# A third staging tile for the spilled pieces of u and of the gates, and accumulating transfers cut at 4 KB instead of 8 KB

## The chip, the cores and the metric

The kernel runs on 1 core of one Trainium2 chip. The metric is the time of one execution in device microseconds (us). Engines are named as the profile names them: PE multiplies, PEld is its weight load, DVE, ACT and POOL compute, and SP only queues transfers. ACT and POOL queue transfers too; such rows read ACTq and POOLq, or DMA_DIRECT2D on POOL. All transfers share 16 DMA engines.

## The reference

One decoder block on 1024 tokens of width 1024, with 16 meta tokens put ahead. All in float32:

```python
h = rmsnorm(concat([meta, x]), norm_g)
u_pool, z_pool, q, k, v, z_attn, f_logit, g_pool, g_attn = split(h @ w_in)
y_pool = causal_multiscale_pool(u_pool, pool_w, pool_scale) * silu(z_pool)
log_f = log_sigmoid(f_logit + b_forget)
y_attn = forgetting_attention(q, k, v, log_f) * silu(z_attn)   # 8 heads of 64, causal
merged = sigmoid(g_pool) * (y_pool @ w_up_pool) + sigmoid(g_attn) * (y_attn @ w_up_attn)
out = rmsnorm(x + merged @ w_out, final_norm_g)
```

## The kernel before, in words

Every product is made of three products of rounded parts (high with high, high with low, low with high), so PE has three matmuls for each. PE's order is written out by hand; the order on the other engines comes from a scheduler.

From about 60 to 430 us the kernel runs 16 attention units (4 head pairs, 2 heads, 2 halves of 512 queries). A unit's scores go through `qk`, then `maxes` takes the maximum over the keys (line 726): DVE transposes the running maxima into the tile `mt` (line 729), reduces it, and a few small copies and one more transposition spread the result; then `soft` exponentiates block by block and `av` multiplies with V. `finish` (line 778) copies the unit's sum into the tile `t`, and SP stores its two halves in DRAM (`sp_y`, line 788). For the last head pair one half is stored.

Between these matmuls PE works off "fill": projections of the input, 24 matmuls to a piece, in chunks of 128 output columns. The projections of q, k and v stay on the chip. Those of u (`f_u`, 4 chunks of 3 pieces) and of 12 gate chunks (`f_raw`, 2 pieces each) are spilled: ACT copies the piece from PSUM into a staging tile `st` of the pool `stg`, which has two, and SP stores it (`sp_u`, `sp_gp`, `sp_ga`). A piece can go into a staging tile only when the store of the piece before last has landed. Fill pieces alternate between two PSUM banks, so a bank must be emptied before the piece after next begins.

Meanwhile sums of blocks of the input and of the weights are made in DRAM by transfers alone. ACT queues copies from DRAM to DRAM (`move`, line 605, rows with `td` and `gs`), one or two of them between the exponentials of a unit; POOL queues transfers that add one DRAM block to another (`add` and `add_y`, lines 614 and 641), 17 transfers of 0.5 to 1.5 MB each, 18.35 MB in all.

Each transfer that SP or ACT queues has one of eight completion semaphores (DMAHW0 to DMAHW7 in the program's rows), dealt out in turn; the queueing engine first waits until the transfer that had this one before, eight transfers back, has landed.

From about 430 us on PE multiplies without a break (products of sums of blocks, then the up and output projections). At that point `F.drain()` has run the last fill pieces, the attention pools are closed, and new tiles (`bp`) take their place.

Of the kernel before, what the change touches and what calls it, by code (L numbers as in the profile page):

```python
# [8 lines left out]
F32 = mybir.dt.float32  # L9
F32R = mybir.dt.float32r  # L10
AF = mybir.ActivationFunctionType
ALU = mybir.AluOpType
# [10 lines left out]
KB = 128  # L23
# [30 lines left out]
def tile_hybrid_block(ctx, tc, x, meta, norm_g, w_in, b_forget, pool_w, pool_scale,  # L54
                      w_up_pool, w_up_attn, w_out, final_g, out):
    nc = tc.nc
# [19 lines left out]
    stg = ctx.enter_context(tc.tile_pool(name="stg", bufs=2))  # L76
# [3 lines left out]
    ap_ = A.enter_context(tc.tile_pool(name="ap", bufs=1))  # L80
# [36 lines left out]
    def behind(ins, prev):  # L117
        tc.add_manual_dep(ins.ins, prev.ins.name,
                          mybir.DependencyInfo(mybir.DependencyClass.Sync, mybir.DependencyReason.DATA),
                          reason="wait")  # L120
# [41 lines left out]
    def w_chunk(col, **kw):  # L162
        return split_w([w_in2[:, :, col:col + 128]], **kw)
# [20 lines left out]
    def g_proj(w, t0, t1):  # L184
        wh, wl = w
        ps = fill_bank()[:, :t1 - t0]
        yield from g_mm3(ps, [(wh[:, k, :], wl[:, k, :], hh[k][:, t0:t1], hl[k][:, t0:t1]) for k in range(KO)])
        return ps
# [69 lines left out]
    def keys_of(t0, t1):  # L258
        r = [(0, min(t1, SEQ) - t0, t0 + NM)]
        if t1 > SEQ:  # L260
            r.append((SEQ - t0, t1 - t0, 0))
        return [(slice(a, b), slice(d, d + b - a)) for a, b, d in r]
# [72 lines left out]
            if c0:  # L335
                yield from v_blocks(p, *{384: (1, 2), 768: (3, 4, 5)}[c0])

    spill, stores, evacs = {}, [], []

    def f_raw(key, col):  # L340
        w = w_chunk(col)
        dt = dr.tile([128, SEQ], F32, name=f"sp_{key[0]}{key[1]}")
        spill[key] = dt
        for c0, c1 in HALVES:
            ps = yield from g_proj(w, c0, c1)
            st = stg.tile([128, 512], F32, name="st")
            evacs.append(nc.scalar.activation(st, ps, AF.Copy))
            stores.append(nc.sync.dma_start(dt[:, c0:c1], st))

    def f_u(g):  # L350
        w = w_chunk(COL_U + g * 128)
        dt = dr.tile([128, L], F32, name=f"sp_u{g}")
        spill["u", g] = dt
        for c0, c1 in PIECES:
            ps = yield from g_proj(w, c0, c1)
            st = stg.tile([128, 512], F32, name="st")[:, :c1 - c0]
            nc.scalar.activation(st, ps, AF.Copy)
            for c, d in keys_of(c0, c1):
                last = nc.sync.dma_start(dt[:, d], st[:, c])
            stores.append(last)  # L360

    class Fill:
# [3 lines left out]
        def add(self, name, g, gate=0, apart=False):  # L366
            self.must.append((name, g, gate, apart))
# [245 lines left out]

    def add(dst, src):
        d, r = [t.rearrange("r c -> (r c)").rearrange("(p m) -> p m", m=2048) for t in (dst, src)]
        behind(nc.gpsimd.dma_start(d, r, accum_op=ALU.add, max_dma_last_dim=8192), trs[-1])

    trs = []

# [20 lines left out]

    def add_y(p):
        d, r = [spill[n, p].rearrange("(p k) c -> p (k c)", k=2) for n in ("y", "y2")]
        behind(nc.gpsimd.dma_start(d, r, accum_op=ALU.add, max_dma_last_dim=8192), trs[-1])

    SUMS = {
        0: [(put_h, "11")],
        1: [(add, HS["11"], HS["l11"]), (n21, 0), (put, TD[1], WB["11"]), (put, TD[5], WB["12"])],
        2: [(add, TD[1], TD[5]), (n21, 1), (put_h, "22")],
        3: [(add, HS["22"], HS["l22"]), (n21, 2), (put, TD[3], WB["22"])],
        4: [(add, TD[3], TD[5]), (n21, 3), (put_g, GS[1], GB["11"])],  # L650
        5: [(add, HS["X"], HS["11"]), (n12, 0), (put_g, GS[5], GB["12"])],
# [23 lines left out]
    class Unit:  # L675
# [49 lines left out]

        def maxes(self, extra=0.0, hook=None):
            F.pull(LM1 + extra)
            mt = ap_.tile([KB, 512], F32, name="mt")
            tr = nc.vector.transpose(mt, self.m)
            if hook is not None:  # L730
                hook(tr)
            r, r2 = self.m[:, :16], self.m[:, 16:32]
            x, y, mx = [sm.tile([128, 16], F32, name=n) for n in ("mx", "my", "mz")]
            nc.vector.tensor_reduce(r, mt.rearrange("p (j b) -> p j b", b=32), axis=AX.X, op=ALU.max)
            for a, b in ((0, 64), (64, 0)):
                nc.scalar.activation(x[a:a + 64], r[b:b + 64], AF.Copy)
            nc.vector.tensor_tensor(r2, r, x, op=ALU.max)
            for a, b in ((0, 32), (32, 0), (64, 96), (96, 64)):
                nc.scalar.activation(y[a:a + 32], r2[b:b + 32], AF.Copy)
            nc.vector.tensor_tensor(mx, r2, y, op=ALU.max)  # L740
            self.pm = psT.tile([128, 512], F32, name="pt")
            nc.vector.transpose(self.pm, mx[:, :, None].to_broadcast([128, 16, 32]))
            F.pull(LM2)
# [62 lines left out]
    for g in (3, 2, 1, 0):  # L806
        F.add_free(f_u(g))
    for key in raws:
        F.add_free(f_raw(key, cols[key[0]] + 128 * key[1]))
# [10 lines left out]
    def sums_at(i, tr):  # L820
        trs.append(tr)
        sums_of(i)
        if i % 4 == 1 and i > 1:
            add_y(i // 4 - 1)
# [664 lines left out]
```

## Time and profile before

| what | value |
|---|---|
| time, median of 3 runs | 721.52 us (720.6 to 723.17) |
| the profiled execution's own time | 722.44 us |
| its span in the trace | 720.4 us |
| PE busy | 707.4 us, 98% of the span |
| DVE, ACT, POOL busy | 512.0, 425.9 and 353.9 us |

The span is the time between the first and the last instruction on the chip; 2.0 us of the execution's time lie outside it. A busy time is a sum over an engine's instructions. Where PE is busy nearly all the time, only its gaps, and what sets their ends, can be saved or added to.

### The profile page before, as it was taken

The page shows a single profiled execution, that of the slowest core. Times are in us where ns is not written, and L with a number is a line of the kernel's source. Part 1 is how long each engine was busy: PE and PEld are TensorE (multiplying, and loading weights), DVE is VectorE, ACT ScalarE, POOL GpSimd, SP SyncE. Part 2 cuts the span into 40 slices and gives each one's busy share as a digit, 9 for nine tenths or more (in the row PEclk, how much of TensorE's full clock was granted, in tenths as well). Part 3 has the DMA queues.
Part 4 walks back from the last instruction along what each step waited for, and adds up shares of the span by engine and source line. Part 5 has one row for each costly group of instructions (what it writes and reads, how often), then busy time and mean ns, then how long its engine had stood idle before and what let it go on. Part 6 is the DMA issues. An engine that isn't in the chain of part 4 may idle for free.

```text
span 720.4 us, 10921 instructions
## 1 busy us (share of the span) xinstructions
PE 707.4 (98%) x3613; PEld 610.7 (85%) x3613; DVE 512.0 (71%) x909; ACT 425.9 (59%) x936; POOL 353.9 (49%) x481
## 2 busy tenths in 40 slices
PE   8999999799999999999999999999999999999996
PEld 6997999798889988898888888888888888888885
DVE  5743488477688767787587866899847545888775
ACT  7753577567787867777587614455646332535445
POOL 5412336477377675747388643458951010007152
PEclk9999999999999999999999999999999999999999
DMA  9211225986968889497858768799518366861006
GB/s 308 65 30 30 60 62 199 271 244 193 260 177 230 239 229 281 118 261 214 224 154 206 223 202 318 239 304 308 129 35 273 113 224 233 272 224 60 0 1 233
DMA packets 97482, 134.09 MB, mean 186 GB/s; under 512 B 11809, under 2 KB 63009, under 8 KB 95154
## 3 DMA queue, kind: packets, MB, share of 16 engines
q1 hardware_dynamic: 83296, 94.07, 40.8%
q0 software_dynamic: 2512, 18.35, 13.3%
q10 hardware_dynamic: 11618, 20.98, 8.2%
q8 instruction: 28, 0.46, 0.2%
q14 instruction: 28, 0.23, 0.1%
HBM read 103.29 MB, written 62.59 MB: 230 GB/s over the span
## 4 chain that ended last, share of the span: by engine, by line
PE 94%; ACT 2%; DMA 2%; DVE 1%; issue 1%; POOL 0%; POOLq 0%; ACTq 0%
PE pj L170 55%; PE pj L1049 12%; PE pj L1369 8%; PE po L775 5%; PE pt L1049 4%; PE pt L1369 2%; PE ps L711 2%; DMA sp_u<-st 2%; PE ps L710 2%; PE pj L521 1%; PE pt L232 1%; PE pj L711 1%; PE pj L710 1%; ACT qa L268 1%; PE pn L232 0%
## 5 line engine op out<-in xcount | busy, mean ns | idle before, releaser
L170 PE MATMUL pj<-hh,whi 128*128 128x512 f32 (+3 forms) x576 | 128.3, 350 | 0.0
L170 PE MATMUL pj<-hh,wlo 128*128 128x512 f32 (+3 forms) x576 | 127.1, 346 | 0.0
L170 PE MATMUL pj<-hl,whi 128*128 128x512 f32 (+3 forms) x576 | 126.8, 345 | 0.0
L170 PEld LDWEIGHTS pj<-hh,whi 128*128 128x128 f32 x576 | 98.4, 190 | 10.2 <-ACT hh L234 0.4
L158 POOL TENSOR_TENSOR wlo<-raw,whi 128x256 fp32r<-128x256 f32 x100 | 73.5, 774 | 65.1 <-PE pj L170 24.5
L170 PEld LDWEIGHTS pj<-hh,wlo 128*128 128x128 f32 x576 | 96.8, 188 | 10.0
L765 POOL TENSOR_TENSOR acc<-acc,S 128x256 f32<-128x256 f32 (+2 forms) x128 | 90.3, 723 | 30.5 <-ACT S L752 20.8
L170 PEld LDWEIGHTS pj<-hl,whi 128*128 128x128 f32 x576 | 96.6, 189 | 9.8
L757 DVE TENSOR_TENSOR pl<-S,ph 128x512 fp32r<-128x512 f32 (+4 forms) x112 | 80.5, 736 | 19.4 <-ACT ph L756 18.9
L1011 POOL TENSOR_TENSOR gw<-graw,gw 128x256 fp32r<-128x256 f32 x52 | 53.6, 1056 | 44.2 <-ACT gw L1004 41.8
L1049 PE MATMUL pj<-gh,gw 128*128 128x512 f32 x276 | 64.3, 389 | 0.0
L724 DVE TENSOR_TENSOR pt<-pt,S 128x400 f32<-128x400 f32 (+2 forms) x96 | 46.4, 483 | 22.1 <-ACT S L715 19.6
L1049 PEld LDWEIGHTS pj<-gh,gw 128*128 128x128 f32 x276 | 51.8, 188 | 10.9
L752 ACT ACTIVATE S<-S 128x512 f32<-128x512 f32 (+4 forms) x112 | 50.6, 479 | 8.6 <-DVE S L751 8.4
L756 ACT ACTIVATE ph<-S 128x512 fp32r<-128x512 f32 (+4 forms) x112 | 52.4, 482 | 2.3 <-PE po L775 1.4
L751 DVE TENSOR_TENSOR S<-S,pt 128x512 f32<-128x512 f32 (+4 forms) x112 | 49.7, 498 | 0.6
L1262 DVE TENSOR_TENSOR rl<-pj,rl 128x512 f32<-128x512 f32 x32 | 22.0, 689 | 28.7 <-PE pj L170 28.1
L1004 ACT ACTIVATE gw<-graw 128x512 fp32r<-128x512 f32 x38 | 23.5, 626 | 27.9 <-DMA graw<-gs 12.0
L715 ACT ACTIVATE S<-ps,negc 128x16 f32<-128x16 f32 (+4 forms) x65 | 33.0, 513 | 10.9 <-PE ps L711 10.3
L765 POOL TENSOR_TENSOR acc<-S 128x256 f32<-128x256 f32 (+1 forms) x32 | 28.6, 926 | 21.1 <-ACT S L752 17.5
L136 POOL TENSOR_TENSOR X<-G 128x256 f32<-128x256 f32 x8 | 5.8, 740 | 63.9 <-DVE G L1264 63.9
L775 PE MATMUL po<-ph,V 128*128 128x512 f32 (+4 forms) x112 | 36.6, 327 | 0.3 <-ACT ph L756 0.2
(250 smaller groups left out, 1434.2 us busy)
## 6 DMA issues: line engine op xcount, KB each, us to landing
raw<-in_w_in_dram SPq DMA_DIRECT2D x27, 512.0 KB, 5.9
gs<-in_w_in_dram ACTq DMA_DIRECT2D x15, 512.0 KB, 7.6
gs<-gs POOLq DMA_DIRECT2D x4, 1536.0 KB, 12.7
graw<-gs SPq DMA_DIRECT2D x12, 512.0 KB, 6.1
td<-in_w_out_dram ACTq DMA_DIRECT2D x10, 512.0 KB, 11.4
graw<-in_w_in_dram SPq DMA_DIRECT2D x9, 512.0 KB, 6.9
xt<-in_x_dram SPq DMA_DIRECT2D x8, 512.0 KB, 6.3
accd<-acc SPq DMA_DIRECT2D x16, 256.0 KB, 4.2
```

The source lines that it names most:

```text
L158: ins = nc.gpsimd.tensor_tensor(lo[:, k:k + 2], raw[:, k:k + 2], r32(hi[:, k:k + 2]), op=ALU.subtract)
L170: nc.tensor.matmul(ps, a, b, start=(i == 0), stop=(i == len(seq) - 1))
L724: nc.vector.tensor_tensor(m[:kb, c0:], m[:kb, c0:], s[:kb, c0:], op=ALU.max)
L751: nc.vector.tensor_tensor(s[:kb, c0:], s[:kb, c0:], self.pm[:kb, c0:], op=ALU.subtract)
L752: exps.append(nc.scalar.activation(s[:kb, c0:], s[:kb, c0:], AF.Exp))
L756: nc.scalar.activation(ph[:kb, c0:], s[:kb, c0:], AF.Copy)
L757: dves.append(nc.vector.tensor_tensor(pl[:kb, c0:], s[:kb, c0:], r32(ph[:kb, c0:]), op=ALU.subtract))
L765: accs.append(nc.gpsimd.tensor_tensor(acc[:kb, c:c1], (S0 if b == 1 else acc)[:kb, c:c1], s[:kb, c:c1], op=ALU.add))
L775: nc.tensor.matmul(self.po[:, c0:], v, self.P[b][i][:kb, c0:], start=(b == 0 and i == 0), stop=(b == self.nb - 1 and i == 1))
L1011: nc.gpsimd.tensor_tensor(op[:, 1, k:k + 2], raw[:, k:k + 2], r32(op[:, 0, k:k + 2]), op=ALU.subtract)
L1049: nc.tensor.matmul(ps, stat(n, i, p, k), op_h[n][q][k // 2][:, k % 2], start=fresh and m == 0, stop=m == 11, skip_group_check=True)
L1369: nc.tensor.matmul(ps, pick(A_, k, p)[:, i * 128:(i + 1) * 128], pick(B_, k, q)[:, c0:c1], start=start and n == 0, stop=n == 11, skip_grou ...
```

## The change

The pieces of u and of the gates go through three staging tiles in turn instead of two. The third is a tile of the attention pool `ap`, and its 2 KB per partition come from `mt`, which now shares the buffer of `t` (tag "t"). The transfers that add are cut into pieces of at most 4096 bytes instead of 8192.

```diff
-    spill, stores, evacs = {}, [], []
+    spill, stores, evacs, staged = {}, [], [], [0]
+
+    def stage_in():
+        staged[0] += 1
+        if staged[0] % 3:
+            return stg.tile([128, 512], F32, name="st")
+        return ap_.tile([128, 512], F32, name="st", bufs=1)
...
-            st = stg.tile([128, 512], F32, name="st")
+            st = stage_in()
...
-            st = stg.tile([128, 512], F32, name="st")[:, :c1 - c0]
+            st = stage_in()[:, :c1 - c0]
...
-        behind(nc.gpsimd.dma_start(d, r, accum_op=ALU.add, max_dma_last_dim=8192), trs[-1])
+        behind(nc.gpsimd.dma_start(d, r, accum_op=ALU.add, max_dma_last_dim=4096), trs[-1])
...
-        behind(nc.gpsimd.dma_start(d, r, accum_op=ALU.add, max_dma_last_dim=8192), trs[-1])
+        behind(nc.gpsimd.dma_start(d, r, accum_op=ALU.add, max_dma_last_dim=4096), trs[-1])
...
-            mt = ap_.tile([KB, 512], F32, name="mt")
+            mt = ap_.tile([KB, 512], F32, name="mt", tag="t")
```

Line numbers after the change are 6 higher from `f_raw` on. The order of the instructions on PE, ACT and DVE stays as it was; on POOL only the shape of the adding transfers differs, and on SP one pair of stores moves at the end of the fill. What the instructions wait for does change.

The first place is ACT in the second attention unit, where the last two pieces of the u chunk 1 (`st_1646`, `st_1700`) are staged while the copies `td1` and `td5` are queued. SP's store of `st_1646` stands there in the program like this, before and after, with semaphore 4:

```order
L609 DMA hsX_802<-neg_1671 128x512 [waits DMAHW2_49,Activation_49,Pool_49]
L609 DMA hsA_799<-neg_1671 128x512 [waits DMAHW3_49]
L359 DMA sp_u1_1505<-st_1646 128x384 [waits DMAHW4_49,Activation_49]
L788 DMA sp_y0_773<-t_1728 64x512 [waits DMAHW5_49,Activation_49]
L788 DMA sp_y20_774<-t_1728 64x512 [waits DMAHW6_49]
```

ACT before:

```order
L612 DMA td1_781<-in_w_out_dram 256x512 [waits DMAHW7_49]
L756 ACTIVATE ph_1785<-S_1446 128x400 [waits Activation_49]
L357 ACTIVATE st_1700<-pj_1649 128x272 [waits PE_49]
L752 ACTIVATE S_1550<-S_1550 128x272 [waits DVE_49]
L612 DMA td1_781<-in_w_out_dram 256x512 [waits DMAHW1_49]
L756 ACTIVATE ph_1810<-S_1550 128x272 [waits Activation_49]
L752 ACTIVATE S_1550<-S_1550 128x144 [waits DVE_49]
L612 DMA td5_785<-in_w_out_dram 256x512 [waits DMAHW4_49]
L715 ACTIVATE S_1733<-pj_1734,negc_120 128x512 [waits PE_49,Pool_49]
```

ACT after, at the same place:

```order
L618 DMA td1_781<-in_w_out_dram 256x512 [waits DMAHW7_49]
L762 ACTIVATE ph_1785<-S_1446 128x400 [waits Activation_49]
L363 ACTIVATE st_1700<-pj_1649 128x272 [waits DMAHW5_49,DMAHW3_49,PE_49]
L758 ACTIVATE S_1550<-S_1550 128x272 [waits DVE_49]
L618 DMA td1_781<-in_w_out_dram 256x512 [waits DMAHW1_49]
L762 ACTIVATE ph_1810<-S_1550 128x272 [waits Activation_49]
L758 ACTIVATE S_1550<-S_1550 128x144 [waits DVE_49]
L618 DMA td5_785<-in_w_out_dram 256x512 [waits DMAHW4_49]
L721 ACTIVATE S_1733<-pj_1734,negc_120 128x512 [waits PE_49,Pool_49]
```

The staging copies wait for other, older stores than before; the copy `td5` waits for DMAHW4, the store of `st_1646`, in both.

The second place is DVE in the unit whose maxima are transposed at 313.78 us of the trace. Before:

```order
L724 TENSOR_TENSOR pt_3795<-pt_3795,S_3892 128x144 [waits DVE_49]
L724 TENSOR_TENSOR pt_3795<-pt_3795,S_3926 128x16 [waits DVE_49]
L729 STREAM_TRANSPOSE mt_4002<-pt_3795 128x512 [waits DVE_49]
L734 TENSOR_REDUCE pt_3795<-mt_4002 128x16 [waits DVE_49]
L290 TENSOR_TENSOR ka_3778<-pj_3854,ka_3778 64x384 [waits PE_49,Activation_49]
```

After:

```order
L730 TENSOR_TENSOR pt_3795<-pt_3795,S_3892 128x144 [waits DVE_49]
L730 TENSOR_TENSOR pt_3795<-pt_3795,S_3926 128x16 [waits DVE_49]
L735 STREAM_TRANSPOSE mt_4002<-pt_3795 128x512 [waits DMAHW3_49,DMAHW2_49,DVE_49]
L740 TENSOR_REDUCE pt_3795<-mt_4002 128x16 [waits DVE_49]
L290 TENSOR_TENSOR ka_3778<-pj_3854,ka_3778 64x384 [waits PE_49,Activation_49]
```

The transposition into `mt` now also waits for the two stores of `t` (`sp_y`) of the unit before; behind it on DVE stands `ka_3778`, one of the two that empty a fill piece's PSUM bank (`pj_3854`). The same new wait stands at 14 of the 16 transpositions.

The third place is SP at the end of the fill, where the last two gate pieces are stored and the sums of the exponentials (`accd`) are loaded. Before:

```order
L348 DMA sp_ga2_5017<-st_5174 128x512 [waits DMAHW4_49,Activation_49]
L955 DMA zp_5264<-accd_771 128x1024 [waits DMAHW5_49]
L955 DMA zp_5266<-accd_771 128x1024 [waits DMAHW6_49]
L348 DMA sp_ga3_5187<-st_5213 128x512 [waits DMAHW7_49,Activation_49]
L348 DMA sp_ga3_5187<-st_5241 128x512 [waits DMAHW0_49,Activation_49]
```

After:

```order
L354 DMA sp_ga2_5017<-st_5174 128x512 [waits DMAHW4_49,Activation_49]
L354 DMA sp_ga3_5187<-st_5213 128x512 [waits DMAHW5_49,Activation_49]
L354 DMA sp_ga3_5187<-st_5241 128x512 [waits DMAHW6_49,Activation_49]
L961 DMA zp_5264<-accd_771 128x1024 [waits DMAHW7_49]
L961 DMA zp_5266<-accd_771 128x1024 [waits DMAHW0_49]
```

The two loads now stand behind the two stores, the second of which stores the last piece of the fill.

## Rows read from the trace of the kernel before

**Rows 1.** The page's first part: busy time, share of the span, instructions.

```profile
PE 707.4 (98%) x3613; PEld 610.7 (85%) x3613; DVE 512.0 (71%) x909; ACT 425.9 (59%) x936; POOL 353.9 (49%) x481
```

**Rows 2.** Stretches: length, busy us of PE, PEld, DVE, ACT, POOL; clock; DMA; GB/s.

```profile
136.40:140.50 4.10, 0.02 (x1) 0.00 (x0) 0.00 (x0) 0.70 (x2) 0.00 (x0) 1.00 1.05 375
140.50:144.50 4.00, 3.96 (x12) 3.66 (x13) 2.10 (x3) 3.31 (x7) 0.84 (x2) 0.57 1.07 306
```

**Rows 3.** Timeline, 130 to 146 us: start, length, engine, line, instruction, [idle before, releaser].

```profile
135.91 0.51 PE L170 MATMUL pj<-hh,wlo 128*128 128x384 f32 x2
140.53 0.50 PE L710 MATMUL pj<-qa,ka 128*128 128x512 f32 x1 [4.11 <-ACT S L715]
...
131.94 0.31 ACT L752 ACTIVATE S<-S 128x144 f32<-128x144 f32 x1
139.19 0.50 ACTq L612 DMA_DIRECT2D td<-in_w_out_dram  x1
139.79 0.69 ACT L715 ACTIVATE S<-pj,negc 128x512 f32<-128x512 f32 x1 [7.55 <-DMA sp_u<-st]
```

**Rows 4.** SP's store of `st_1646`: timeline, its landing, and the usual landing.

```profile
128.03 0.32 SPq L359 DMA_DIRECT2D sp_u<-st  x1
DMA to landing us min/median/max: 11.1/11.1/11.1
sp_u<-st SPq DMA_DIRECT2D x8, 192.0 KB, 2.7
```

**Rows 5.** The page's part on queues: the adding transfers' queue, whole span.

```profile
q0 software_dynamic: 2512, 18.35, 13.3%
```

**Rows 6.** DMA queues from 131 to 136 us: packets, MB, share of 16 engines.

```profile
q0 software_dynamic: 98, 0.80, 87.1%
q1 hardware_dynamic: 63, 0.10, 6.2%
q10 hardware_dynamic: 38, 0.08, 5.6%
```

**Rows 7.** The same from 302 to 308 us.

```profile
q0 software_dynamic: 136, 1.11, 89.8%
...
q1 hardware_dynamic: 137, 0.07, 5.8%
```

**Rows 8.** Stores of `t` from 299.6 us: SP's row, landing of both, then 258.5 us.

```profile
L788 SPq DMA_DIRECT2D sp_y<-t x2: 451/564/676, 299.7 to 300.2; - x2
DMA to landing us min/median/max: 16.3/16.8/17.4
...
DMA to landing us min/median/max: 14.7/14.7/14.7
```

**Rows 9.** Timeline of DVE and PE around two transpositions into `mt`.

```profile
273.03 0.72 DVE L729 STREAM_TRANSPOSE mt<-pt 128x512 f32<-128x512 f32 x1
...
313.78 0.72 DVE L729 STREAM_TRANSPOSE mt<-pt 128x512 f32<-128x512 f32 x1
315.26 1.13 DVE L290 TENSOR_TENSOR ka<-pj,ka 64x384 fp32r<-64x384 f32 x2
...
317.63 1.57 PE L170 MATMUL pj<-hh,whi 128*128 128x384 f32 x8
```

**Rows 10.** Timeline after the fill, SP, DVE and PE; last a row of the chain.

```profile
425.81 1.32 SPq L955 DMA_DIRECT2D zp<-accd  x2
433.01 1.25 DVE L960 STREAM_TRANSPOSE zp<-zp 128x1024 f32<-128x1024 f32 x1 [7.77 <-DMA zp<-accd]
...
452.35 0.69 DVE L1060 TENSOR_TENSOR za<-pj,za 128x512 f32<-128x512 f32 x1
...
429.93 1.07 PE L1049 MATMUL pj<-hh,gw 128*128 128x512 f32 x4
...
452.12 8.16 PE pj L1049 x36
```

**Rows 11.** POOL's instruction for an adding transfer, by line (duration min/median/max).

```profile
L616 POOL DMA_DIRECT2D gs<-gs x4: 800/812/821, 256.3 to 382.0; - x4
```

## The prediction

> **What bounds the kernel now.** I read the page's busy times first: PE is busy 98% of the span [rows 1], so a gain or a loss is a change of PE's gaps. Next I looked for the gaps in the timeline of PE. From 60 us to the end there is one long one: after the two matmuls that start at 135.91 PE does nothing until 140.53, and the trace puts 4.11 us of idle down to ACT's line 715 [rows 3]. The table by stretches shows what it costs besides: in the 4.0 us after it the granted clock averages 0.57, so part of the stretch ran at 1.2 GHz instead of 2.4, after an engine that had stood still for 4.1 us [rows 2]. At the full level the same work would have taken 4.0 x 0.57 = 2.3 us, so 1.7 us were lost to the clock. The gap and the clock are worth 4.1 + 1.7 = 5.8 us; nothing else on PE after 60 us is worth 1 us.
>
> Who caused the gap? ACT had been idle 7.55 us before line 715, released by the landing of a store `sp_u<-st` [rows 3]. That reads like a wait for a staging tile, and it isn't one. What ran just before line 715 is the issue of a copy `td` at 139.19. In the program's order this `td5` waits for DMAHW4, which SP's store of `st_1646` had before it. That store left at 128.03 and took 11.1 us, to 139.1 [rows 4]: the time at which `td5` leaves. Eight transfers share eight semaphores, and the oldest was slow. Then 0.6 us to the start of line 715, 0.69 us of it, and PE goes on.
>
> Why 11.1 us, where the like usually takes 2.7 [rows 4]? From 136.4 on the DMA share is 1.05 [rows 2], and from 131 to 136 us the adding transfer's queue q0 holds 87.1% of the engines [rows 6].
>
> **The change part by part.**
>
> *The third staging tile.* It takes away waits for staging tiles. Up to 420 us no such wait holds PE, and `td5` keeps its wait for DMAHW4 in the changed program. Its part in the sum is 0. It does free ACT at the end of the fill, but there PE runs from one matmul to the next whatever ACT does [rows 10], so nothing is gained.
>
> *The halved packets.* Whole span: 18.35 MB in packets of 8192 bytes are 2240, and 13.3% of 16 x 720.4 us is 1533 us, so 0.68 us a packet [rows 5]. From 302 to 308 us, 136 packets of q0 take 89.8% of 96 us, 0.63 us each, and q1 gets 137 packets in the same time, 0.04 us each [rows 7]: one of SP's for each of the adding transfer's. A waiting store thus pays a full adding packet before each of its own. The store of `st_1646` has 128 packets of 1536 bytes, 8 for each of 16 engines. From 131 to 136 us q0 pays 69.7 us / 98 = 0.71 us a packet, q1 5.0 / 63 = 0.08 us [rows 6]; with a share for q10 a turn is 0.85 us or so, and 8 turns are 6.8 us of the 11.1.
>
> A packet of 4096 bytes isn't in the trace in this queue. From below, its cost is half, 0.36 us, if it goes by bytes alone; from above 0.71 us, if all of it is fixed per packet. I take half, since the queue's packets already run at nearly one rate by the byte. A turn is then 0.36 us shorter, and 8 turns 2.8 us. The store also starts about 2 us late behind adding packets that were there first; a part of that shrinks too, so I take 3.1 us in all, and the store lands at 136.0 instead of 139.1. At most the whole excess over 2.7 us halves, 4.2 us, which ends the gap; at least nothing changes. PE's gap shrinks by the same amount, from 4.1 to 1.0 us: **3.1 us**, with ends at 0 and 4.1.
>
> The clock: a gap of 1.0 us is nearer to the gaps of a few tenths, after which the clock stays, than to that of 4.1. I take the **1.7 us** back, with 0 as the other end.
>
> On POOL an adding instruction takes 0.8 us whatever its size [rows 11]. Should it double, 17 x 0.8 = 14 us are added to an engine at 49% [rows 1], ahead of sums that no matmul waits for soon; 0, at worst some tenths.
>
> *`mt` in the buffer of `t`.* This is a new wait on DVE: the transposition into `mt` must wait until the stores of `t` of the unit before have landed. These stores go out 14 us or more ahead, and in 11 of the 14 places land 2 us or more before they are wanted. The bad place is the transposition at 313.78 [rows 9]: the second store of 300.2 lands 17.4 us later [rows 8], at 317.6, so 3.8 us too late. The one at 273.03 [rows 9] is late by 0.8, since the stores before it, issued up to 259.2, take 14.7 us [rows 8]. Behind the waiting transposition on DVE stand the reduction and `ka` of line 290, which empties a fill bank: it now ends at 315.26 + 1.13 = 316.4, and PE's piece that takes the bank starts at 317.63 [rows 9]. The slack is 1.2 us; the wait at 273.03 fits in it, 3.8 us would stall PE by 2.6.
>
> Halved packets move this landing less than the other one, for SP's queue has a weight load of 1024 small packets in front, in which most of the addition is served anyhow. By turns: about 10 of those are left for each engine at 302 us, at 0.32 + 0.04 and part of q10; then 8 of a gate store and 8 of `sp_y`, at 0.32 + 0.09 + 0.09 by the sizes of their rows. That is 4 + 8 = 12 us from 302, and 1 to 2 us until it is landed: 315 to 316, 1.2 to 2.2 us after 313.78. PE loses 0 to 1.0 us; I take **0.6 us**, with ends at 0 and 2.6.
>
> *The move on SP.* The first two loads `zp` leave at 425.81 now; after the change they stand behind the store of the last fill piece, whose matmuls end when those of line 1049 begin, at 429.93 [rows 10]. They leave at about 431, 5 us late, and the sum on DVE that starts at 433.01 starts near 438 [rows 10]. Queued behind it on DVE are four more such sums and the eviction at 452.35 [rows 10], for which PE waits when the bank comes round: two products of 2.72 us after 452.12, or 457.5 [rows 10]. 452.35 + 0.69 leaves 4.5 us. DVE idles between these sums and catches up some of the 5 us; 0, at worst 1 us.
>
> *Sum.* 3.1 + 1.7 - 0.6 = 4.2 us off the profiled execution: 722.4 (span 720.4 and 2.0 around it) becomes 718.2. The median of the runs, 721.52, lies 0.9 below that execution, so the prediction is **717.3 us**.
>
> A rule of the Trainium skill speaks against the change. Its page "DMA: Bandwidth & Descriptors", section "Queues, rings and completion order", says that an engine changes between queues only at packets, and that a packet typically holds some 9 to 17 descriptors. If the 8 pieces that an engine has of an addition were one such packet, cutting them would leave a waiting store where it was, and the time would be that of the first rival below, 724.1 us. The trace doesn't agree: 136 against 137 packets is an exchange after every piece.
>
> **The rivals.**
>
> *The packets don't shorten the waits* (the slower side). The turns would have to be by bytes or in larger groups, or a half packet to cost as much as a whole. Then the gap at 136 us stays, and the wait of `mt` at 313.78 costs all of its 2.6 us: 721.5 + 2.6 = 724.1 us. It decides as soon as the stores land later than 315.0, which is 313.78 and the 1.2 us of slack. Against it is the one for one exchange [rows 7]; that no packet of this size is in the trace leaves it open. 14%.
>
> *The gap closes altogether.* If the excess of 8.4 us halves, the store lands at 134.9 and PE doesn't wait: 4.1 + 1.7 = 5.8 us, 715.7 us. For it speaks that the late start counts too; against it that SP's own queue is served in order. 12%.
>
> *Half a gain.* The store lands 1 to 2 us earlier and the clock falls nevertheless, or the wait at 313.78 takes back what the gap gave: 1 to 2 us, 719.5 to 720.5. 16%, nearly all of it within 0.3%.
>
> *The end of the fill becomes a new wait*: the 5 us of delay on DVE are not caught up, and a bank comes too late by 1 us or more. It would join any of the above; some 3% to be slower by it.
>
> **How the numbers follow.** The forecast has 55%, with its own range of 715.8 to 719.2 (the store 2.4 to 4.1 us earlier, 0 to 1 us lost at 313.78). With the rivals the range is 715.0 to 723.0: it leaves out most of the first rival and a little below. A measurement can tell 0.3% from no change, 2.2 us. Faster: 55 + 12, and a little of the half gain, 68%; slower: 14 + 3, less what the first rival has under 2.2 us, 15%; the rest, 17%, within.
>
> **What would show it.** Right: a store from 128.03 that lands in some 8 us, a gap near 136 us of 1 us or less, and a clock of 1.00 from 140 to 145 us; twice as many packets in q0, with about half the time each; the transposition near 309 us (313.78 less the 4.8 us gained before it) 1 to 2 us late, released by `sp_y`. Wrong: the same 11 us of landing, or a PE gap behind line 290 of more than 2 us. If ACT goes on at 132 us without a wait at `td5`, I have misread its cause.

## The result

The changed kernel takes 725.16 us (median of 20 runs, 721.73 to 726.33), the kernel before 722.41 us (20 runs, 720.6 to 723.6). The ratio is 1.003, with a 95% interval of 1.002 to 1.004: slower, by 1.4 to 2.9 us as the interval has it, where the prediction said 717.3 us and faster. The profiled execution took 725.37 us, its span is 723.5 us.

The page's busy times, to set beside [rows 1]:

```profile
PE 708.8 (98%) x3613; PEld 612.1 (85%) x3613; DVE 512.2 (71%) x909; ACT 425.7 (59%) x936; POOL 355.6 (49%) x481
```

The waits of PE between 100 and 720 us, by what ended them (total us, times, longest):

```profile
PE pj L716 <- ACT S L721: 3.8, 1, 3.8
PE pj L1055 <- ACT gw L1010: 1.5, 1, 1.5
PE po L781 <- ACT ph L762: 0.7, 2, 0.6
```

The first wait is the gap of before, 3.8 us instead of 4.1 [rows 3]; the second is new. I set the starts of PE's 3613 matmuls in the two traces side by side, one by one. The changed kernel falls behind by 0.41 us up to 130 us, nearly all of it near 18 us, by 0.40 at 137 to 145 us, 0.43 at 291 us and 1.78 at 485 us; the rest is 0.03, together 3.05 us. The first of these is no effect of the change: it stands in other profiles below too, in code that no edit touches (0.9 up to 130 us with packets of 2 KB, 0.5 with a cut addition).

**Around 136 us.** The timeline of PE and ACT, beside [rows 3]:

```profile
136.32 0.51 PE L170 MATMUL pj<-hh,wlo 128*128 128x384 f32 x2
139.29 0.50 ACTq L618 DMA_DIRECT2D td<-in_w_out_dram  x1
139.89 0.69 ACT L721 ACTIVATE S<-pj,negc 128x512 f32<-128x512 f32 x1 [7.23 <-DMA sp_u<-st]
140.63 0.79 PE L716 MATMUL pj<-qa,ka 128*128 128x512 f32 x1 [3.79 <-ACT S L721]
```

The landing of SP's store of `st_1646`, queued at 128.44 us, beside [rows 4], and the queues from 131 to 136 us, beside [rows 6]:

```profile
DMA to landing us min/median/max: 10.8/10.8/10.8
```

```profile
q0 software_dynamic: 184, 0.75, 81.7%
q1 hardware_dynamic: 116, 0.18, 11.5%
```

`td5` still leaves when that store lands, so the chain of causes was read rightly. But the store lands after 10.8 us instead of 11.1, not after 8. The stretches, beside [rows 2]:

```profile
136.50:140.60 4.10, 0.33 (x2) 0.01 (x1) 0.00 (x0) 0.71 (x2) 0.00 (x0) 0.78 1.04 347
140.60:144.60 4.00, 3.97 (x11) 3.69 (x12) 2.10 (x3) 3.30 (x7) 0.84 (x2) 0.50 1.02 316
144.60:148.60 4.00, 4.00 (x22) 3.82 (x22) 2.31 (x6) 2.99 (x7) 3.17 (x6) 0.87 0.52 198
```

The clock is at its lower level for longer than before: (1 - 0.50) x 4 + (1 - 0.87) x 4 = 2.5 us lost after the gap, where before it was 1.7. That needn't be the change's: experiment 4 below has the same instructions here and lost 1.5.

**Around 300 us** the halved packets did more than was forecast. The queues from 302 to 308 us, beside [rows 7], and the stores of `t` from 300.7 us, beside [rows 8]:

```profile
q0 software_dynamic: 205, 0.84, 70.5%
q1 hardware_dynamic: 758, 0.60, 32.1%
```

```profile
L794 SPq DMA_DIRECT2D sp_y<-t x2: 452/718/983, 300.7 to 301.2; - x2
DMA to landing us min/median/max: 10.8/11.7/12.7
```

They land after 10.8 to 12.7 us instead of 16.3 to 17.4, so the transposition that was to be late isn't. DVE's timeline at the two transpositions of [rows 9]:

```profile
274.62 0.72 DVE L735 STREAM_TRANSPOSE mt<-pt 128x512 f32<-128x512 f32 x1 [0.79 <-DMA sp_y<-t]
...
315.04 0.72 DVE L735 STREAM_TRANSPOSE mt<-pt 128x512 f32<-128x512 f32 x1
```

The one at 315.04 waits for nothing. The one at 274.62 is 0.79 us late, as was worked out (0.8); but that doesn't fit in a slack: it runs on through ACT to the `po` matmul at 292 us, the 0.43 us there. Later profiles put the slack near 0.35 us: 0.3 and 0.2 us of lateness here in experiments 4 and 10 cost PE nothing, 1.3 us in experiment 2 cost it 1.0.

**The end of the fill** is the largest term. The timeline of SP, DVE, ACT and PE, beside [rows 10]; the last two rows are from the kernel before:

```profile
426.33 6.05 SPq L354 DMA_DIRECT2D sp_ga<-st  x3
432.43 0.92 SPq L961 DMA_DIRECT2D zp<-accd  x2
...
437.82 1.25 DVE L966 STREAM_TRANSPOSE zp<-zp 128x1024 f32<-128x1024 f32 x1 [11.32 <-DMA zp<-accd]
...
455.95 0.69 DVE L1066 TENSOR_TENSOR za<-pj,za 128x512 f32<-128x512 f32 x1
...
480.48 1.93 SPq L976 DMA_DIRECT2D fin<-sums  x4
484.76 0.62 DVE L980 TENSOR_REDUCE fin<-fin 128x64 f32<-128x256 f32 x1 [2.07 <-DMA fin<-sums]
...
486.75 1.28 DVE L1066 TENSOR_TENSOR gx<-pj,gx 128x512 f32<-128x512 f32 x2
486.94 0.63 ACT L1010 ACTIVATE gw<-graw 128x512 fp32r<-128x512 f32 x1 [1.09 <-DMA graw<-in_w_in_dram]
...
487.57 7.73 PE L1055 MATMUL pj<-gh,gw 128*128 128x512 f32 x33 [1.54 <-ACT gw L1010]
...
483.50 0.68 DVE L1060 TENSOR_TENSOR gx<-pj,gx 128x512 f32<-128x512 f32 x1
484.60 1.75 PE L1049 MATMUL pj<-gh,gw 128*128 128x512 f32 x7
```

The loads `zp` leave at 432.43 and DVE's first sum starts at 437.82 (forecast: about 431 and near 438). The eviction of the bank, for which I had kept a slack of 4.5 us, is 3.6 us late (455.95 against 452.35) and holds nothing up. But the chain does not end there: the last sum is stored, and SP reads the stored sums back (`fin`), 3.7 us later than before (480.48 against 476.80), of which 1.27 us is the lateness that PE had by then. DVE waits 2.07 us for these reads. Behind its reduction of them, in DVE's order and without a pause, stands the eviction `gx` from a bank `pj`: the first of the two ends at 487.43, and PE, which writes `pj` next, goes on at 487.57. Before, `gx` ended at 484.18 and PE started at 484.60 without waiting.

The row puts PE's wait down to ACT's `gw`, late behind the same reads on SP, which ends at 487.57 too. That is a coincidence of times: in ten of the twelve profiles (both kernels and the ten experiments) the same matmul of PE starts 0.3 to 0.5 us before the same `gw` ends, in experiment 7 after a wait like this one, while in all four that have a wait here (this one and experiments 2, 7 and 10) PE goes on 0.15 us after the end of `gx`. So PE waits for DVE. With these 0.15 us, `gx` had a slack of 0.28 us before.

### The profile page after: what moved, and what is told of

It reads as the page before. It is cut to its first block, busy times and chain, and to the rows that moved or that the text cites. A ratio compares the mean times of both kernels' runs of the same rounds, so it can differ in the third digit from the quotient of the medians.

```text
span 723.5 us, 10931 instructions
## 1 busy us (share of the span) xinstructions
PE 708.8 (98%) x3613; PEld 612.1 (85%) x3613; DVE 512.2 (71%) x909; ACT 425.7 (59%) x936; POOL 355.6 (49%) x481
## 3 DMA queue, kind: packets, MB, share of 16 engines
q0 software_dynamic: 4752, 18.35, 13.7%
## 4 chain that ended last, share of the span: by engine, by line
PE 84%; DMA 7%; ACT 3%; DVE 3%; issue 1%; SPq 1%; POOL 1%; ACTq 0%; POOLq 0%; DVEq 0%
PE pj L170 53%; PE pj L1375 8%; PE pj L1055 6%; PE po L781 5%; PE pt L1375 2%; PE pt L1055 2%; PE ps L717 2%; DMA zp<-accd 2%; PE ps L716 1%; DMA sp_u<-st 1%; DMA xt<-in_x_dram 1%; DMA sums<-ge 1%; PE pj L527 1%; PE pj L717 1%; PE pj L716 1%
## 5 line engine op out<-in xcount | busy, mean ns | idle before, releaser
L170 PEld LDWEIGHTS pj<-hh,whi 128*128 128x128 f32 x576 | 99.1, 192 | 10.1 <-ACT hh L234 0.2
L1055 PEld LDWEIGHTS pj<-gh,gw 128*128 128x128 f32 x276 | 51.7, 188 | 12.7 <-issue 1.9
L721 ACT ACTIVATE S<-ps,negc 128x16 f32<-128x16 f32 (+4 forms) x65 | 33.0, 513 | 11.5 <-PE ps L717 10.8
## 6 DMA issues: line engine op xcount, KB each, us to landing
gs<-gs POOLq DMA_DIRECT2D x4, 1536.0 KB, 14.7
td<-in_w_out_dram ACTq DMA_DIRECT2D x10, 512.0 KB, 11.1
```

The lines of the kernel that those rows point to most:

```text
L170: nc.tensor.matmul(ps, a, b, start=(i == 0), stop=(i == len(seq) - 1))
L1055: nc.tensor.matmul(ps, stat(n, i, p, k), op_h[n][q][k // 2][:, k % 2], start=fresh and m == 0, stop=m == 11, skip_group_check=True)
```

## The experiments

Times stand beside the kernel before on the same chip. The first four take the change apart.

**1. Only the halved packets.**

```diff
-  max_dma_last_dim=8192   (both places, kernel before)
+  max_dma_last_dim=4096
```

> Only the halved packets (4096 bytes), two staging tiles, mt in its own buffer. Theory A (halving reorders what the DMA engines serve, but the last packet of a store still comes when the congestion ends): the time of before within 1 us, the store of st_1646 lands after 10.5 to 11.5 us, PE's gap near 136 us stays at 3.5 to 4.2 us, no gap at 485 us. Theory B (the halving shortens the store by the 3.1 us of the forecast and the other part of the change eats it): 4 to 5 us faster than before, landing in about 8 us, a gap of 1 us or less. Theory C (the small packets themselves cost, by more packets): 1 us or more slower than before.

721.94 us against 722.68: ratio 0.9991, interval 0.9981 to 1.0002. The landing of the store and PE's longest wait from 60 us on:

```profile
DMA to landing us min/median/max: 10.1/10.1/10.1
```

```profile
PE pj L710 <- ACT S L715: 3.1, 1, 3.1
```

Theory A, a little past its edge: the landing is 1.0 us earlier here (10.1 us, 10.5 to 11.5 expected), the gap 3.1 us (3.5 to 4.2 expected), and a measurement can't quite tell the time from no change. The forecast's 3.1 us off the landing and 4.8 us off the time are not there. Nor is theory C's loss of 1 us or more.

**2. Only the third tile, with `mt` in the buffer of `t`, and 3. only `mt` in the buffer of `t`;** both with whole packets.

```diff
   experiment 2, against the changed kernel, both places:
-  max_dma_last_dim=4096
+  max_dma_last_dim=8192
   experiment 3, against the kernel before:
-  mt = ap_.tile([KB, 512], F32, name="mt")
+  mt = ap_.tile([KB, 512], F32, name="mt", tag="t")
```

> Only the third staging tile with mt in the buffer of t; packets of 8192 bytes as before. Theory A (the loss is the order on SP at the end of the fill, 1.7 us, and the wait of mt): the 1.7 us at 485 us are there again; with whole packets the transposition near 314 us waits its 3.8 us and PE loses the 2.6 us of the forecast: 4.5 to 5 us slower than before in all, 726 to 728 us. If the stores of t land early enough with whole packets too: 2 us slower. Theory C (the small packets cost): within 0.5 us of before.

> Only mt in the buffer of t; two staging tiles, packets of 8192 bytes, order on SP as before. Theory A: the wait at 273 us costs PE 0 to 0.5 us and that at 314 us 2.6 us: 2.5 to 3 us slower than before, and no gap at 485 us. Rival (DVE's wait is always covered): within 0.5 us of before.

Experiment 2 took 730.53 us and experiment 3 728.96, both against 722.68: ratios 1.0104 (1.0083 to 1.0124) and 1.0084 (1.0065 to 1.0102). The timeline of DVE and PE at the transposition of 313.78, and a stretch, in experiment 2:

```profile
318.65 0.72 DVE L735 STREAM_TRANSPOSE mt<-pt 128x512 f32<-128x512 f32 x1 [3.88 <-DMA sp_y<-t]
...
321.40 2.90 PE L170 MATMUL pj<-hh,whi 128*128 128x384 f32 x8 [2.58 <-DVE ka L290]
```

```profile
321.40:325.40 4.00, 4.00 (x15) 4.00 (x16) 2.77 (x8) 3.77 (x13) 2.43 (x4) 0.61 0.81 166
```

The same in experiment 3, in the slowest of its 6 runs:

```profile
322.41 0.72 DVE L729 STREAM_TRANSPOSE mt<-pt 128x512 f32<-128x512 f32 x1 [4.21 <-DMA sp_y<-t]
...
325.15 2.88 PE L170 MATMUL pj<-hh,whi 128*128 128x384 f32 x8 [2.91 <-DVE ka L290]
```

With whole packets the wait is what the prediction worked out for them: 3.88 us late (3.8 forecast), PE 2.58 us idle (2.6 forecast) behind line 290. What neither theory had is the clock: 0.61 for the 4 us after it, another 1.6 us. The loss at 291 us, 0.43 in the changed kernel, was 1.0 us in experiment 2 and 2.1 in experiment 3 (matmul by matmul). So both times lie above what was expected, 726 to 728 us for experiment 2 and 2.5 to 3 us of loss for experiment 3. So the shared buffer is dear with whole packets, 6 us in experiment 3, and what the halving does in the changed kernel is to pay for that: the ratio falls from 1.0104 to 1.003, by more than 5 us.

One expectation missed: the 1.7 us at 485 us are not there again in experiment 2's profile, though SP's order is the new one. PE falls behind by 0.5 us there, and its wait is short:

```profile
490.26 2.08 PE L1055 MATMUL pj<-gh,gw 128*128 128x512 f32 x8 [0.18 <-DVE gx L1066]
```

SP's reads of `fin` leave 4.3 us ahead of PE's product before the wait here (482.89, 487.19), 2.7 us ahead in the changed kernel (480.48, 483.16) and 5.1 before (476.80, 481.88). The medians of experiments 2 and 3 still lie 1.6 us apart, the third tile and SP's order together.

**4. The changed kernel with SP's old order, and 7. the kernel before with the new order.**

```diff
   experiment 4, against the changed kernel (of 36 pieces only the last changes its tile):
-  if staged[0] % 3:
+  if staged[0] % 3 or staged[0] > 33:
   experiment 7, against the kernel before (stores[-1] is the last piece's store):
-    last_dve = dves[-1]
+    last_dve, last_st = dves[-1], stores[-1]
...
-        nc.sync.dma_start(zp[k % 2].rearrange("p (u c) -> p u c", u=2), accd[:, 2 * k:2 * k + 2])
+        ld = nc.sync.dma_start(zp[k % 2].rearrange("p (u c) -> p u c", u=2), accd[:, 2 * k:2 * k + 2]); k < 2 and after(ld, last_st)
```

> The changed kernel, but the last three pieces of the fill go through the two old staging tiles, which gives SP's order of before back: the two loads zp ahead of the last two stores. Theory A (that order is what starves PE at 485 us): 1.7 us faster than the changed kernel, some 1 to 1.5 us slower than before, no gap at 485 us. Rival (the gap there comes from the lateness of all that went before, or from the packets): as slow as the changed kernel, about 3 us behind before, and the gap stays.

> The kernel before with nothing changed but SP's order at the end of the fill: the two loads zp stand behind the last two stores, as in the changed kernel. If that order is what starves PE at 485 us: 1.5 to 2 us slower than before, with the gap there behind ACT's line 1004. Rival (it costs only on top of another lateness): within 0.7 us of before.

Experiment 4 took 722.73 us against 722.68 (ratio 1.0005, 0.9992 to 1.0017), where the changed kernel's ratio is 1.003: 1.8 us of it (0.0025 x 722) are SP's order. Experiment 7 took 725.16 against 723.14 (1.003, 1.0016 to 1.0043): the order alone costs 2.0 us, where the whole change costs 2.75. In its profile 1.4 us of loss fall at 486 us; another 0.7 fall at 136 us, which the edit doesn't touch (a gap of 4.8 us in this execution). SP, ACT and PE in experiment 7:

```profile
425.85 7.53 SPq L348 DMA_DIRECT2D sp_ga<-st  x3
433.43 0.93 SPq L955 DMA_DIRECT2D zp<-accd  x2
...
486.50 0.63 ACT L1004 ACTIVATE gw<-graw 128x512 fp32r<-128x512 f32 x1 [1.15 <-DMA graw<-in_w_in_dram]
486.69 3.68 PE L1049 MATMUL pj<-gh,gw 128*128 128x512 f32 x15 [1.15 <-DVE gx L1060]
```

PE is released here by DVE's eviction `gx`, which ends at 486.55. ACT's line 1004 had been expected, but ends at 487.13, after PE has gone on. `gx` stands on DVE behind the reduction of `fin`, so the wait starts at the late sums. In experiment 4 PE's only wait of more than 0.2 us from 60 us on is the one of 136 us:

```profile
PE pj L716 <- ACT S L721: 3.7, 1, 3.7
```

**5. The addition cut short.** Of the addition `hs11 <- hsl11`, 112 of 128 rows are left out; every engine's order stays as before.

```diff
-  1: [(add, HS["11"], HS["l11"]), ...
+  1: [(add, HS["11"], HS["l11"], 16), ...      # rows [:16] of 128; add takes this number (its lines are left out here)
```

> The kernel before, but the addition hs11 <- hsl11 of the second unit takes 16 of its 128 rows of 8192 bytes; the other 112 rows are left out. All else, order and semaphores too, is as before. If that addition is what makes the store of st_1646 slow: it lands in 5 us or less, PE's gap near 136 us and the half clock after it are gone, and the time is 4.1 + 1.7 = 5.8 us below before. Rival (the weight load ahead of the store on SP's queue and the copies of ACT would make it slow anyhow): landing in 8 us or more, gap of 1 us or more, 0 to 4 us faster.

717.09 us against 723.14 (ratio 0.9918, 0.9905 to 0.993): 6.0 us faster. Landing, and the stretch from 136 us:

```profile
DMA to landing us min/median/max: 4.1/4.1/4.1
```

```profile
136.00:140.00 4.00, 4.00 (x22) 3.68 (x21) 2.30 (x4) 3.57 (x7) 0.84 (x2) 1.00 1.09 389
```

So the addition is the cause, and 5.8 us was the right price of gap and clock.

**6. Packets of 2 KB.**

```diff
-  max_dma_last_dim=8192   (both places, kernel before)
+  max_dma_last_dim=2048
```

> Packets of 2048 bytes in the adding transfers, nothing else changed against before. Theory L (a store lands with the last of its packets, on the DMA engine with the most work left, so smaller packets bring the middle packet forward and the last one hardly): the middle packet of the store of st_1646 near 133.5 us, landing after 9.5 to 10.5 us, gap of 2.8 to 3.8 us, 0 to 2 us faster than before, as with 4096 bytes. Turn theory (each packet waits for one adding packet): landing in 8 us or less, gap under 1.5 us, 4 us faster. Cost theory: if packets of this size take more than half of the time of 4096 bytes, q0's share rises above 14% and the time above that of 4096 bytes.

720.31 us against 723.14 (ratio 0.9963, 0.9948 to 0.9978), 2.8 us faster; more than theory L had, less than the turn theory. Landing, PE and stretches of its profile, which took 723.2 us, the slowest of its 6 runs:

```profile
DMA to landing us min/median/max: 9.1/9.1/9.1
```

```profile
139.32 0.50 PE L710 MATMUL pj<-qa,ka 128*128 128x512 f32 x1 [2.04 <-ACT S L715]
```

```profile
139.30:143.30 4.00, 3.25 (x11) 2.57 (x12) 0.70 (x1) 2.06 (x5) 0.22 (x1) 0.64 1.09 314
143.30:147.30 4.00, 4.00 (x14) 3.80 (x13) 3.21 (x5) 3.46 (x8) 2.64 (x4) 0.51 1.00 334
```

The middle packet of the store starts 5.9 us after the store is queued, no sooner than with 4 KB (6.0 in the changed kernel; 8.0 before), at 134.75 us where theory L had about 133.5. The landing shrinks by 2.0 us and the gap by as much, and this execution gave all of that back: (0.36 + 0.49) x 4 = 3.4 us at the lower clock instead of 1.7. How often that happens, a single profile can't say; the median suggests that most runs kept the gain. The queue's row also prices the packets:

```profile
q0 software_dynamic: 9232, 18.35, 14.6%
```

14.6% of 16 x 721.4 us are 1685 us for 18.35 MB, against 1533 with whole packets [rows 5]: the smaller ones cost the DMA engines 10% more, which no wait of PE shows.

**8 and 9. The copy `td5` a unit later,** with packets of 4 KB and of 8 KB. The staging tiles and `mt` are as before; ACT no longer queues `td5` at 132 us, and the addition that needs it moves one unit back.

```diff
-  1: [(add, HS["11"], HS["l11"]), (n21, 0), (put, TD[1], WB["11"]), (put, TD[5], WB["12"])],
-  2: [(add, TD[1], TD[5]), (n21, 1), (put_h, "22")],
-  3: [(add, HS["22"], HS["l22"]), ...
+  1: [(add, HS["11"], HS["l11"]), (n21, 0), (put, TD[1], WB["11"])],
+  2: [(n21, 1), (put, TD[5], WB["12"]), (put_h, "22")],
+  3: [(add, TD[1], TD[5]), (add, HS["22"], HS["l22"]), ...
```

> Two staging tiles, mt in its own buffer, packets of 4096 bytes, and the copies td5 queued one unit later (their addition two places later on POOL), so that ACT doesn't stand at 132 us. If the slow landing costs only through what stands behind it on ACT: the landing of the store stays at 10 to 11 us, the gap near 136 us and the half clock are gone, 716 to 718 us, 5 to 6 us faster than before. Rival (the wait moves to the next transfer on ACT or SP in the same crowd of transfers): a new gap of 2 us or more, 719 to 723 us.

> As the run with td5 one unit later, but packets of 8192 bytes: what the halving is worth once nothing on ACT stands behind the slow store. If nothing: 716 to 717 us, as with packets of 4096 bytes. Rival (other waits, that of the stores of t among them, still cost PE with whole packets): 0.5 to 2 us more than with the halved packets run on the same chip.

With 4 KB 716.42 us against 723.14 (ratio 0.9907, 0.9895 to 0.992), with 8 KB 716.46 against 722.36 (0.9919, 0.9905 to 0.9933): 6 to 6.7 us faster than before. With 4 KB, the landing of the store, the stretch from 136 us and PE's waits from 60 us on:

```profile
DMA to landing us min/median/max: 11.2/11.2/11.2
```

```profile
136.00:140.00 4.00, 4.00 (x23) 3.73 (x22) 2.10 (x3) 2.38 (x6) 3.00 (x5) 1.00 1.03 330
```

```profile
PE po L775 <- ACT ph L756: 0.2, 1, 0.2
```

The store lands as late as ever and PE doesn't notice: only the instruction behind the wait mattered. And once it is out of the way the halving shows no gain: 716.42 and 716.46 us. These are two chips, but the ratios to before differ by less than their intervals, too.

**10. The changed kernel with both repairs:** three tiles, `mt` in the buffer of `t`, 4 KB, `td5` a unit later, the last three pieces through the old tiles.

```diff
-  if staged[0] % 3:
+  if staged[0] % 3 or staged[0] > 33:
...
-  2: [(add, TD[1], TD[5]), (n21, 1), (put_h, "22")],
+  2: [(n21, 1), (put, TD[5], WB["12"]), (put_h, "22")],
...
```

> The changed kernel (three staging tiles, mt in the buffer of t, packets of 4096 bytes) with both repairs: td5 one unit later, and the last three pieces through the old staging tiles. If the third tile brings PE nothing and the wait of mt costs some tenths: 716.4 to 717.2 us, the same as or a little above the kernel with two tiles. Rival (the third tile frees ACT and gains once the gap is gone): 0.5 us or more below 716.4 us.

716.88 us against 722.36 (ratio 0.9924, 0.991 to 0.9937), 0.4 us above experiment 9 on the same chip. The third tile shows no gain with the gap out of the way; the kernel of experiment 8 or 9, with two tiles, is the best of those tried. Its profile, the slowest of the 5 runs, has a wait for `gx`, though SP's order is the old one:

```profile
479.91 8.41 PE L1055 MATMUL pj<-gh,gw 128*128 128x512 f32 x36 [0.67 <-DVE gx L1066]
```

There the reads of `fin` left in time (4.7 us ahead of PE's product before the wait), and DVE's reduction started 5.4 us after them, where it was 4.4 in experiment 9 and 4.3 in the changed kernel. So SP's order isn't all that decides whether `gx` is late; what made these reads slow stays open.

## Why the prediction was wrong

**What bounds the kernel: right.** The wait of `td5` for a semaphore held by a slow store, the addition as the cause, and the price of 5.8 us: experiment 5 measured 6.0, experiments 8 and 9 6 to 6.7.

**The halved packets, 3.1 us: mis-sized, and the main miss.** "The store lands at 136.0 instead of 139.1" failed: it landed 0.3 us sooner after its start in the changed kernel, 1.0 in experiment 1, 2.0 with 2 KB. Over all profiles with `td5` in its old place the landing was 11.1, 11.3, 11.4 and 11.8 us with whole packets (before, experiments 2, 3 and 7) and 10.1, 10.7 and 10.8 with half packets (experiments 1 and 4 and the changed kernel): the halving took some 0.9 us off it, not 3.1. The price of a packet was not the fault: 13.7% of 16 x 723.5 us for 4480 packets is 0.35 us, and I took 0.36. For a packet in the middle the exchange of turns held at 4 KB: in the trace's packet records 63 of the store's 128 packets had started by 136.0 us before and 105 after, and the middle one came at 134.4 instead of 136.1. But the last one started at 138.1 instead of 138.0. I worked out a sum of turns that fits a packet in the middle (with 2 KB not even that: it came no sooner than with 4 KB), and a transfer has landed with its last. Why the last one moved so little isn't shown. My reading is one DMA engine that came to the store last, having the most queued ahead; it is argued from the tail of the records (the last three packets start 0.46 us apart, about one turn of 0.35 + 0.08), since the trace doesn't name the engine of a packet, and other profiles with 4 KB don't all have such a tail (experiment 1 hasn't). At 300 us the same halving took 4.7 us off the later landing (17.4 to 12.7), twice what I had allowed, and those stores had two additions beside them, queued at 298.3 and 298.9 us, the first of 1.5 MB where the one at 127 us has 1 MB: more of the addition was still to come when the store's turns were over. That fits, but no run varied it, and at a third place, the store of `t` at 259 us, no gain stands out: 14.7 us before, 13.3 in experiment 2 with whole packets, 14.0 in the changed kernel.

The rule of the Trainium skill that was weighed (page "DMA: Bandwidth & Descriptors", section "Queues, rings and completion order") would have left a waiting store where it was at either place. In experiment 1, where the packet size alone was changed, the landings at 300 us went from 16.3 to 17.4 us down to 10.7 to 12.2, which speaks against it here.

**The clock, 1.7 us back: didn't come,** since the gap stayed.

**The wait of `mt`, 0.6 us: about the right size, at the other place.** 313.78 cost nothing and 273.03 cost 0.43. The step "the wait at 273.03 fits in it" failed: I used the slack of the bank at 316 us for a place where the late result goes through ACT to the matmuls of V. For whole packets the working of the second place held to a tenth in experiment 2 and to 0.4 us in experiment 3, without the clock that fell after it. The 0.43 is that of one execution: experiments 4 and 10, with the same buffer and packets, lost nothing at 291 us.

**The move on SP, "0, at worst 1 us": wrong, and what made the sign.** It cost 1.8 us in the profile and 2.0 us in experiment 7. The delays of the loads and of DVE were as forecast; the step that failed is the search for who waits. I followed the late sums to the first eviction behind them on DVE, found a slack of 4.5 us, and stopped. The sums' own result goes through two more transfers on SP, the store and the reads of `fin`, and behind the reduction of what was read stands a later eviction on DVE, `gx`, whose slack was 0.28 us.

**The third tile, 0:** no gain was seen (experiments 4 and 10), as forecast.

So the terms in the two profiles are 0.3 us for the gap less 0.7 for a longer spell at the lower clock, -0.4 for `mt` and -1.8 for SP's order, and an early difference of 0.4 that isn't the change's. Of these, SP's order is the one that the medians show by itself (1.8 and 2.0 us in experiments 4 and 7); with the old order the changed kernel was level with the kernel before. Of the rivals, the first had the gap right (it stays) and the wait of `mt` wrong; the end of the fill, which had 3%, is the one that came, by a route that I hadn't drawn. The upper end of the forecast's own range, 719.2, doesn't follow from the terms it names: 721.5 less 2.4 + 1.7 - 1.0 is 718.4. The result lies above both, and above the 723.0 of the whole range.

## What to carry to other kernels

A transfer's landing is set by its last packet: smaller packets on a competing queue brought the middle forward by 2 us here and the landing by 0.9, so don't price a landing by its middle packet. Better, take the waiting instruction out of the way (experiment 8 gained 6.7 us with the store as slow as ever). When an instruction is moved past another on a queue that runs in order, follow its result to the end, through every later transfer of that chain and everything queued behind each, not to the first consumer with slack. Check the releaser that a profile names where two candidates end at the same time: another execution, in which they end apart, tells which it was. And a buffer shared to make room carries the other user's landing with it: with slow stores in front, `mt` in the buffer of `t` cost 6 us.

## What the hardware showed that I had not expected

What a stall costs is more than its length once the clock falls with it. A gap of 1.54 us at 487 us left the granted clock at 1.00 in the stretch after it:

```profile
487.50:491.50 4.00, 3.93 (x17) 3.30 (x18) 4.00 (x4) 2.00 (x5) 2.80 (x2) 1.00 1.06 389
```

The gaps at 136 us, of 2.04 to 4.82 us, and those of 2.58 and 2.91 us at 321 and 325 us in experiments 2 and 3 were each followed by a stretch in which the clock was at 1.2 GHz for a part of the time or all of it (means over 4 us from 0.50 to 0.65). But a gap of 2.18 us in experiment 3, at 295 us, was not:

```profile
295.34:299.34 4.00, 4.00 (x20) 3.48 (x21) 4.00 (x9) 3.32 (x11) 3.76 (x7) 1.00 0.00 0
```

So the length of the gap doesn't decide alone. Nor did the loss go with it: 3.4 us after a gap of 2.04 (experiment 6), 2.5 after 3.79 (changed kernel), 1.5 after 3.71 (experiment 4), 1.7 after 4.11 (before) and after 4.82 (experiment 7). An execution with a shorter gap can so end later than one with a longer.
